# Recurrent mixer: the 64 token level's block products issued first, the 32 token level's directly behind them

## The chip, the cores and the metric

One core of one Trainium2 chip runs the whole program. The metric is the device time of one execution in microseconds (us). Matrix products run on TensorE (PE in the profile, its weight loads are PEld), elementwise work on VectorE (DVE), activations and copies on ScalarE (ACT), some elementwise work on GpSimd (POOL), and DMAs are issued mostly by SyncE (SP). Each engine works through its own queue in order; semaphores tie the queues together.

## The reference, cut to what matters

The model is an encoder trunk of two layers over 1024 tokens of width 1024. Layer 0 mixes tokens by windowed attention, layer 1 by a bidirectional gated linear recurrence (HGRN2); each layer also has four cross-attention heads and ends with a ConvGLU channel mixer. The change touches the recurrence of layer 1 alone:

```python
def gla_chunked(q, k, v, log_f):
    ...
    b = jnp.cumsum(log_f, axis=2)
    b_end = b[:, :, -1:]
    q_dec = q * jnp.exp(b)
    k_dec = k * jnp.exp(-b)
    k_end = k * jnp.exp(b_end - b)
    causal = np.tril(np.ones((HG_CHUNK, HG_CHUNK), dtype=bool))
    s = jnp.where(causal, jnp.einsum('bcthk,bcshk->bchts', q_dec, k_dec), 0.0)
    o_intra = jnp.einsum('bchts,bcshv->bcthv', s, v)

    def step(state, inp):
        qd, ke, vc, dec = inp
        o = jnp.einsum('bthk,bhkv->bthv', qd, state)
        state = dec[..., None] * state + jnp.einsum('bshk,bshv->bhkv', ke, vc)
        return state, o
    ...

o = (gla_chunked(q, k_f, v, lf_f)
     + flip_t(gla_chunked(flip_t(q), flip_t(k_b), flip_t(v), flip_t(lf_b))))
```

There are 8 heads of 128 keys and 128 values, a forward and a backward pass, and in each pass a token sees the values of the tokens before it (or behind it) weighted by a product of decays. The sums are exact whatever the chunk length is.

## The kernel before, in words

The program runs `start` (norms and memory keys), `window` (layer 0's mixer), an output projection, `ffn(0)`, then `hgrn` (layer 1's mixer), an output projection and `ffn(1)`. The tile framework orders each engine's queue when the program is built: a planner walks through time by a cost model, and of the instructions that are ready on an engine takes the one that stands earliest in the program text. An instruction of later text is taken where no earlier one is ready. The order that results is fixed in the program.

`hgrn` goes head by head (`head(h, cur)`, then `proj(h + 1)`). `proj` computes a head's queries `q`, forget inputs `f` and `b`, and for pairs of heads the values and gates, as products of the normed activations (`uh`, `ul`) with weights (`wh`, `wl`), in groups of 24 matmuls of 512 columns in fp32r into a PSUM tile `pj` (three matmuls per block: L84, L85, L86). Two `pj` banks exist. The rest of `hgrn` uses plain fp32, in which each `pe.matmul` becomes two instructions.

`head` calls `direction` four times, for (pass d, half b) = (0, 0), (1, 1), (0, 1), (1, 0); a half is 512 tokens, four blocks of 128. So there are 32 directions in all. One direction works like this, everything laid out as 128 keys by 512 tokens:

- ACT and DVE turn the forget input into log decays, sum them within chunks of 16 tokens (L1026) and take exponentials: `EP` (decay from the start of the chunk) and `ER` (decay to its end).
- L1054: four fp32 matmuls write the 128 by 128 score blocks `pa[:, c, :]` for chunks of 16 tokens and their pairs.
- The score blocks between further chunks are written over this by levels. For n = 32 and n = 64, `step(n // 2)` lengthens the decays (L1060 and L1061 on DVE, in place), then a tile `G` is filled, one half of it by POOL (L1068), the other by DVE (L1069), and L1074 multiplies its halves: for n = 32 there are 8 matmuls (16 instructions) that write 32 partitions each, for n = 64 there are 4 (8 instructions) that write 64 partitions each. They use a part of the array's columns, by `tile_position`. In the text the 32 token level stands first, and its matmuls stand ahead of `step(32)`.
- `step(64)`, then POOL takes out the total decay `dec` (L1080) and makes `qin` (L1082), to which DMAs of later weights are tied, and DVE makes `ER * k` (L1083).
- DVE copies the causal part of `pa` into `Az` (L1084), which ACT or POOL puts into `As` (L1088, L1090).
- PE transposes `ER * k` (L1093), ACT copies it (L1095), PE forms the state updates `pu` (L1098), and ACT and DVE run the states `S` (L1105, L1107).

After four directions `output` sums `po` from `As`, `qin` and `S` (L1122), norms and gates it and transposes it back (L1132). In heads 2, 4, 6 and 7 `cross` puts units of cross attention in between (transposes at L220, products through L84 to L86).

Tiles from `E()` share five buffers. A direction takes eight of them: `a_`, `L1`, `R`, `B`, `E1`, `E2`, and `G` of each level. A buffer is free again when the last reader of its tile is done; for a `G` that is the last matmul of its level at L1074. `pa` has two banks, shared with the scores of the cross attention.

Of the kernel before, what the change touches and what calls it, by code (L numbers as in the profile page):

```python
# [16 lines left out]
P = 128  # L17
# [32 lines left out]
def build(tc, A, out):  # L50
    nc = tc.nc
    act, dve, pool, pe = nc.scalar, nc.vector, nc.gpsimd, nc.tensor
# [824 lines left out]
    def hgrn():  # L877
# [4 lines left out]
        late = tc.alloc_tile_pool(name="hgv", bufs=1, side="right", reuse_waits="tile")  # L882
        V, G = [late.tile([P, 3, NT, P], F32, name=x) for x in ("v", "gs")]
        wp = tc.alloc_tile_pool(name="hg1", bufs=1, side="right", reuse_waits="tile")
# [4 lines left out]
        def bank(tag, shape=(P, 4, P)):  # L889
            return psp.tile(list(shape), F32, tag=tag, bufs=PB[tag], name=tag)  # L890
# [46 lines left out]
        def proj_tm(h, us, ts):  # L937
# [3 lines left out]
            for t in ts[::2]:  # L941
# [10 lines left out]
                for x in range(2):  # L952
                    g = G[:, two, t + x, :]
                    with tc.high_priority(AHEAD):
# [24 lines left out]
        def proj(h):  # L979

            r = {"q": [None, None], "s": [[None, None], [None, None]], "v": V[:, h % 3], "gs": G[:, h % 3], "marks": []}
            us = {}
# [21 lines left out]
        def direction(h, r, d, b, qin, S, As):  # L1004
# [5 lines left out]
            def E():  # L1010
                return early.tile([P, 512], F32, tag="E", bufs=5, name="E")

            def halves(x, n):
                x = x.rearrange("p (b a c) -> p b a c", a=2, c=n)
                return x[:, :, lt, :], x[:, :, er, :]
# [19 lines left out]
            pa = bank("pa")  # L1035
# [6 lines left out]
            def parts(n):  # L1042
                return halves(EP, n) + halves(ER, n) + halves(q, n) + halves(k, n)
# [12 lines left out]
            def step(n):  # L1056
                pl_, pe_, rl_, re_ = parts(n)[:4]
                e = 0 if d else n - 1
                nb = 512 // (2 * n)
                dve.tensor_tensor(re_, re_, bc(pl_[:, :, e:e + 1], [P, nb, n]), op=ALU.mult)  # L1060
                dve.tensor_tensor(pl_, pl_, bc(pe_[:, :, e:e + 1], [P, nb, n]), op=ALU.mult)  # L1061

            for n in (32, 64):
                step(n // 2)
                G = E()
                gl, ge = halves(G, n)
                pl_, pe_, rl_, re_, ql, qe, kl, ke = parts(n)
                pool.tensor_tensor(gl, pl_, ql, op=ALU.mult)  # L1068
                dve.tensor_tensor(ge, re_, ke, op=ALU.mult)  # L1069
                for c in range(4):  # L1070
                    for i in range(64 // n):
                        o = i * 2 * n
                        lo, eo = o + lt * n, o + er * n
                        pe.matmul(pa[eo:eo + n, c, lo:lo + n], G[:, c * P + eo:c * P + eo + n],  # L1074
                                  G[:, c * P + lo:c * P + lo + n], start=True, stop=True,
                                  tile_position=(0, eo))
            step(64)
            dec = wp.tile([P, 4], F32, tag="dec", bufs=2, name="dec")
            e = 0 if d else P - 1
# [71 lines left out]
        def head(h, r):  # L1151
            qin = [wp.tile([P, T], F32, tag=f"qin{d}", bufs=1, name="qin") for d in range(2)]
            S = [wp.tile([P, NT, P], F32, tag=f"S{d}", bufs=1, name="S") for d in range(2)]
            As = [None, None]
            for i, (d, b) in enumerate(((0, 0), (1, 1), (0, 1), (1, 0))):
                direction(h, r, d, b, qin[d], S[d], As)
                if i < len(r["later"]):
                    r["run"](r["later"][i])
                cross(HX[h][i])
                if h == 7 and i == 2:  # L1160
                    wo1.early(psj, 2, es)
            if h == 7:
                wo1.more(r["marks"], es)
                early.release()
                es.release()
                eq.release()
                wo1.w1 = tc.alloc_tile_pool(name="wa1", bufs=2, reuse_waits="tile")
                with tc.issue_after(r["marks"][2].ins):
                    wo1.load(0)
                wo1.open(2, 0)  # L1170
            for i, b in enumerate((1, 0)):
                output(h, r, b, qin, S, As)
                cross(HX[h][4 + i])
# [132 lines left out]
```

## Time and profile before

| | us |
|---|---|
| median of three runs (2729.33 to 2731.97) | 2729.53 |
| span of the profiled execution | 2732.3 |
| of it ahead of `hgrn` (to 1252) | 1252 |
| `hgrn` and the start of the output projection (1252 to 1940) | 688 |
| the rest (1940 to 2732) | 792 |
| PE busy over the span | 2661.3 |
| DVE busy | 1824.4 |
| ACT busy | 1391.2 |
| POOL busy | 468.6 |

The profiled execution's own span is 2.8 us above the median of the timed runs. Matmuls overlap in the pipeline: a matmul of 512 columns shows a duration of 0.39 us, while in a dense stretch the next one starts 0.227 us after it. What a matmul costs is read from the distance between starts, not from durations. In the timeline a row merges neighbours of one line; a row of L1074 gives the shape of its first instruction, so "128*32 ... x24" is a stretch that holds 16 instructions of the 32 token level and 8 of the 64 token level.

### The profile page before, as it was taken

The page shows a single profiled execution, that of the slowest core. Times are in us where ns is not written, and L with a number is a line of the kernel's source. Part 1 is how long each engine was busy: PE and PEld are TensorE (multiplying, and loading weights), DVE is VectorE, ACT ScalarE, POOL GpSimd, SP SyncE. Part 2 cuts the span into 40 slices and gives each one's busy share as a digit, 9 for nine tenths or more (in the row PEclk, how much of TensorE's full clock was granted, in tenths as well). Part 3 has the DMA queues.
Part 4 walks back from the last instruction along what each step waited for, and adds up shares of the span by engine and source line. Part 5 has one row for each costly group of instructions (what it writes and reads, how often), then busy time and mean ns, then how long its engine had stood idle before and what let it go on. Part 6 is the DMA issues. An engine that isn't in the chain of part 4 may idle for free.

```text
span 2732.3 us, 37483 instructions
## 1 busy us (share of the span) xinstructions
PE 2661.3 (97%) x13496; PEld 2231.1 (82%) x13496; DVE 1824.4 (67%) x3031; ACT 1391.2 (51%) x2550; POOL 468.6 (17%) x517
## 2 busy tenths in 40 slices
PE   8999999999999999999999999999899999999998
PEld 7888887788888888877888888888788788888886
DVE  6588777678556565488686767868566856556456
ACT  6367667544444445455444545545454544444453
POOL 1231120211111100032222231312121111110012
PEclk9999999999999999999999999999999999999999
DMA  8683213656777856673235531111466677775656
GB/s 282 207 186 75 66 49 97 204 183 154 199 205 187 206 155 232 204 249 124 86 124 127 117 78 55 55 47 34 133 219 170 165 202 204 197 206 159 222 192 219
DMA packets 213579, 428.45 MB, mean 157 GB/s; under 512 B 20368, under 2 KB 77072, under 8 KB 207760
## 3 DMA queue, kind: packets, MB, share of 16 engines
q1 hardware_dynamic: 187264, 333.50, 37.8%
q0 software_dynamic: 23680, 88.09, 15.6%
q10 hardware_dynamic: 2448, 4.46, 0.4%
q8 instruction: 106, 1.74, 0.3%
q14 instruction: 81, 0.66, 0.1%
HBM read 333.17 MB, written 117.96 MB: 165 GB/s over the span
## 4 chain that ended last, share of the span: by engine, by line
PE 84%; DVE 8%; DMA 3%; ACT 2%; issue 2%; POOL 1%; SPq 0%; DVEq 0%; POOLq 0%; ACTq 0%
PE X L541 25%; PE V L541 11%; PE pj L84 7%; PE pj L85 7%; PE pj L86 7%; PE Y L541 5%; PE pb L84 4%; PE pb L85 4%; PE pb L86 3%; PE po L1122 1%; PE pt L341 1%; PE pa L1074 1%; PE pa L1054 1%; DVE wl L80 1%; DVE wl L90 1%
## 5 line engine op out<-in xcount | busy, mean ns | idle before, releaser
L90 DVE TENSOR_TENSOR wl<-st,wh 128x1024 fp32r<-128x1024 f32 (+1 forms) x234 | 258.6, 1110 | 338.3 <-ACT wh L89 331.1
L89 ACT CAST wh<-st 128x1024 fp32r<-128x1024 f32 (+1 forms) x234 | 219.1, 938 | 291.4 <-PE X L541 180.4
L84 PE MATMUL pj<-uh,wh 128*128 128x512 f32 x512 | 206.6, 404 | 6.4 <-DVE xl L90 4.6
L541 PE MATMUL X<-wl,wh 128*128 128x512 f32 x528 | 205.6, 391 | 0.6 <-DVE wl L90 0.6
L541 PE MATMUL X<-wh,wl 128*128 128x512 f32 x528 | 205.7, 391 | 0.0
L541 PE MATMUL X<-wh 128*128 128x512 f32 x528 | 201.0, 391 | 4.0 <-DVE c L850 3.8
L86 PE MATMUL pj<-uh,wl 128*128 128x512 f32 x512 | 203.4, 398 | 0.0
L85 PE MATMUL pj<-ul,wh 128*128 128x512 f32 x512 | 202.7, 396 | 0.1
L84 PE MATMUL pj<-wh,uh 128*128 128x384 f32 (+1 forms) x512 | 190.2, 372 | 0.4 <-DVE v L283 0.4
L85 PE MATMUL pj<-wl,uh 128*128 128x384 f32 (+1 forms) x512 | 186.3, 364 | 0.0
L86 PE MATMUL pj<-wh,ul 128*128 128x384 f32 (+1 forms) x512 | 186.1, 364 | 0.0
L80 DVE TENSOR_TENSOR wl<-st,wh 128x1024 fp32r<-128x1024 f32 (+1 forms) x93 | 115.9, 1252 | 28.0 <-ACT wh L79 27.1
L541 PE MATMUL V<-uh,wh 128*128 128x512 f32 x344 | 133.9, 389 | 0.3 <-ACT uh L89 0.3
L541 PE MATMUL V<-ul,wh 128*128 128x512 f32 x344 | 134.0, 389 | 0.0
L541 PE MATMUL V<-uh,wl 128*128 128x512 f32 x344 | 133.9, 389 | 0.0
L79 ACT CAST wh<-st 128x1024 fp32r<-128x1024 f32 (+1 forms) x103 | 104.0, 1016 | 49.0 <-PE pj L85 27.2
L541 PEld LDWEIGHTS X<-wh 128*128 128x128 f32 x528 | 99.5, 189 | 25.9 <-issue 4.6
L84 PEld LDWEIGHTS pj<-uh,wh 128*128 128x128 f32 x512 | 97.3, 190 | 26.6 <-DVE xl L90 5.5
L1068 POOL TENSOR_TENSOR E<-EP,q 128x256 f32<-128x256 f32 x64 | 54.4, 851 | 372.0 <-DVE EP L1061 286.7
L541 PEld LDWEIGHTS X<-wl,wh 128*128 128x128 f32 x528 | 99.5, 189 | 21.9 <-DVE wl L90 1.0
L541 PEld LDWEIGHTS X<-wh,wl 128*128 128x128 f32 x528 | 99.4, 188 | 20.9
L86 PEld LDWEIGHTS pj<-uh,wl 128*128 128x128 f32 x512 | 97.0, 190 | 19.6
(337 smaller groups left out, 7328.7 us busy)
## 6 DMA issues: line engine op xcount, KB each, us to landing
st<-hid SPq DMA_DIRECT2D x154, 256.0 KB, 3.4
st<-in_ffw_dram SPq DMA_DIRECT2D x106, 256.0 KB, 3.5
w2s<-in_ffw_dram POOLq DMA_DIRECT2D x24, 1024.0 KB, 8.0
st<-in_ffw_dram SPq DMA_DIRECT2D x48, 512.0 KB, 3.7
hid<-tt SPq DMA_DIRECT2D x88, 256.0 KB, 4.6
st<-w2s SPq DMA_DIRECT2D x88, 256.0 KB, 3.2
sx<-in_ffw_dram SPq DMA_DIRECT2D x80, 256.0 KB, 4.0
sy<-in_ffw_dram SPq DMA_DIRECT2D x40, 512.0 KB, 5.8
```

Source lines behind the costliest of these rows:

```text
L79: act.copy(h[:, :n], raw)
L80: (eng or dve).tensor_tensor(l[:, :n], raw, h[:, :n].bitcast(F32), op=ALU.subtract)
L84: pe.matmul(o, ah, bh, start=first, stop=False)
L85: pe.matmul(o, ah, bl, start=False, stop=False)
L86: pe.matmul(o, al, bh, start=False, stop=last)
L89: act.copy(h, src)
L90: dve.tensor_tensor(l, src, h.bitcast(F32), op=ALU.subtract)
L341: pe.transpose(tp[:, j, :], sm[:, j, c * P:(c + 1) * P], ident)
L541: pe.matmul(o, x, y, start=new, stop=e, skip_group_check=not first)
L1054: pe.matmul(pa[:, c, :], E2[:, cs], E1[:, cs], start=True, stop=True)
L1068: pool.tensor_tensor(gl, pl_, ql, op=ALU.mult)
L1074: pe.matmul(pa[eo:eo + n, c, lo:lo + n], G[:, c * P + eo:c * P + eo + n], G[:, c * P + lo:c * P + lo + n], start=True, stop=True, tile_pos ...
```

## The change

The loop over n now only fills the two `G` tiles, with the same DVE and POOL instructions in the same text order as before. The matmuls move into a function `blocks(n)`, which is called for 64 first. `tc.issue_after(x)` adds an ordering edge, without a semaphore, from `x` to each instruction of the block that runs on the same engine: every matmul of the 32 token level comes behind the last one of the 64 token level in PE's queue. No instruction is added or taken away, and each matmul has the same operands and the same target as before.

```diff
+            Gs = {}
             for n in (32, 64):
                 step(n // 2)
-                G = E()
-                gl, ge = halves(G, n)
+                Gs[n] = E()
+                gl, ge = halves(Gs[n], n)
                 pl_, pe_, rl_, re_, ql, qe, kl, ke = parts(n)
                 pool.tensor_tensor(gl, pl_, ql, op=ALU.mult)
                 dve.tensor_tensor(ge, re_, ke, op=ALU.mult)
+
+            def blocks(n):
+                G = Gs[n]
                 for c in range(4):
                     for i in range(64 // n):
                         o = i * 2 * n
                         lo, eo = o + lt * n, o + er * n
-                        pe.matmul(pa[eo:eo + n, c, lo:lo + n], G[:, c * P + eo:c * P + eo + n],
-                                  G[:, c * P + lo:c * P + lo + n], start=True, stop=True,
-                                  tile_position=(0, eo))
+                        last = pe.matmul(pa[eo:eo + n, c, lo:lo + n], G[:, c * P + eo:c * P + eo + n],
+                                         G[:, c * P + lo:c * P + lo + n], start=True, stop=True,
+                                         tile_position=(0, eo))
+                return last
+
+            with tc.issue_after(blocks(64).ins):
+                blocks(32)
             step(64)
```

## The prediction

> **What bounds the kernel now.** I read the page's busy times and its chain first, then the table by stage, then PE's timeline inside `hgrn`.
>
> ```profile
> PE 2661.3 (97%) x13496; PEld 2231.1 (82%) x13496; DVE 1824.4 (67%) x3031; ACT 1391.2 (51%) x2550; POOL 468.6 (17%) x517
> PE 84%; DVE 8%; DMA 3%; ACT 2%; issue 2%; POOL 1%; SPq 0%; DVEq 0%; POOLq 0%; ACTq 0%
> 1252.00:1940.00 688.00, 678.13 (x4133) 568.97 (x4133) 516.28 (x1029) 346.97 (x757) 175.12 (x188) 1.00 0.28 81
> ```
>
> PE is busy 97% of the span and makes 84% of the chain that ended last. The third row is the stage of the change: PE is busy 678 of 688 us, DVE (the third pair) 516, ACT 347, POOL 175, and the granted clock is 1.00. So in this stage time follows what PE's queue costs, and a later result on DVE or ACT costs something only where PE then runs dry. Busy time can't show what a short matmul costs, since pipelined durations overlap. I read that from distances between starts in PE's timeline: how much later the stream of projections goes on when a stretch of L1074 stands in it.
>
> **What the change does to PE's queue.** No matmul comes or goes. What can change is in how many stretches the 24 instructions of a direction stand, and the order inside. Before, the 32 token level is ready several us ahead of the 64 token level, and the planner uses its matmuls to fill short holes. The first and the last stretch of the stage:
>
> ```profile
> 1280.20 0.31 PE L1074 MATMUL pa<-E 128*32 128x32 f32 x6
> ...
> 1929.65 0.92 PE L1074 MATMUL pa<-E 128*32 128x32 f32 x14
> ```
>
> Between these two the timeline shows L1074 in 58 stretches for 32 directions. 15 directions stand in one stretch of 24; the other 17 hold 26 boundaries too many. I counted three kinds: 10 cuts inside a level with projections between, 6 places where projections lie exactly between the two levels, and 10 cuts where only 128 column fp32 work (transposes, `po`) lies between.
>
> **The price of a stretch.** Four stretches between dense fp32r matmuls:
>
> ```profile
> 1279.65 0.39 PE L85 MATMUL pj<-ul,wh 128*128 128x512 f32 x1
> 1279.88 0.39 PE L86 MATMUL pj<-uh,wl 128*128 128x512 f32 x1
> ...
> 1280.44 0.50 PE L84 MATMUL pj<-wh,uh 128*128 128x512 f32 x1
> ...
> 1281.24 0.39 PE L84 MATMUL pj<-wh,uh 128*128 128x512 f32 x1
> ...
> 1284.42 0.39 PE L86 MATMUL pj<-wh,ul 128*128 128x512 f32 x1
> ```
>
> ```profile
> 1399.29 0.39 PE L86 MATMUL pj<-uh,wl 128*128 128x512 f32 x1
> 1399.52 1.05 PE L1054 MATMUL pa<-E 128*128 128x128 f32 x8
> 1400.50 0.45 PE L1074 MATMUL pa<-E 128*32 128x32 f32 x16
> ...
> 1401.68 0.39 PE L84 MATMUL pj<-uh,wh 128*128 128x512 f32 x1
> ```
>
> ```profile
> 1890.28 0.40 PE L85 MATMUL pj<-ul,wh 128*128 128x512 f32 x1
> 1890.60 0.68 PE L1074 MATMUL pa<-E 128*64 128x64 f32 x8
> ...
> 1892.01 0.40 PE L86 MATMUL pj<-uh,wl 128*128 128x512 f32 x1
> ```
>
> ```profile
> 1559.31 0.39 PE L86 MATMUL pj<-uh,wl 128*128 128x512 f32 x1
> 1559.53 1.05 PE L1054 MATMUL pa<-E 128*128 128x128 f32 x8
> 1560.52 1.05 PE L1074 MATMUL pa<-E 128*32 128x32 f32 x24
> 1561.50 0.50 PE L84 MATMUL pj<-uh,wh 128*128 128x512 f32 x1
> ...
> 1562.30 0.39 PE L84 MATMUL pj<-uh,wh 128*128 128x512 f32 x1
> ```
>
> The yardstick: from 1281.24 to 1284.42 there are 14 steps, so a dense projection matmul takes 0.227 us. A 128 column fp32 instruction takes 0.112 us, from this row of the chain (2.46 / 22):
>
> ```profile
> 1361.28 2.46 PE po L1122 x22
> ```
>
> In each case I take the time from the last projection ahead to the fourth behind, minus 4 x 0.227 = 0.91, minus 8 x 0.112 = 0.90 where L1054 stands in it. Six instructions of the 32 token level: 1281.24 - 1279.88 - 0.91 = 0.45. All 16: 1401.68 - 1399.29 - 0.91 - 0.90 = 0.58. The 64 token level's 8: 1892.01 - 1890.28 - 0.91 = 0.82. All 24 in one: 1562.30 - 1559.31 - 0.91 - 0.90 = 1.18. So each further instruction of 32 costs (0.58 - 0.45) / 10 = 0.013, and entering and leaving a stretch costs 0.45 - 6 x 0.013 = 0.37 us. Both levels apart cost 0.58 + 0.82 = 1.40 against 1.18 together: 0.22 saved where only the seam between the levels closes.
>
> For cuts with fp32 work between:
>
> ```profile
> 1716.43 1.05 PE L1054 MATMUL pa<-E 128*128 128x128 f32 x8
> 1717.41 0.38 PE L1074 MATMUL pa<-E 128*32 128x32 f32 x10
> 1717.72 0.66 PE L1132 MATMUL pt<-ident,on 128*128 128x128 f32 x4
> 1718.31 0.92 PE L1074 MATMUL pa<-E 128*32 128x32 f32 x14
> 1719.16 0.66 PE L1093 MATMUL pt<-ident,ER 128*128 128x128 f32 x4
> ```
>
> From L1054's start to the instruction behind the products: 1719.16 - 1716.43 - 12 x 0.112 = 1.39. Uncut, at 1559.53: 1561.50 - 1559.53 - 0.90 = 1.07. One such cut costs 0.3 us.
>
> If every direction stood whole: 10 x 0.37 + 6 x 0.22 + 10 x 0.3 = 8.0 us.
>
> **What of it is left.** The edge orders the levels, it doesn't glue them. The 32 token level follows at once only while nothing of earlier text is ready. Such an edge is in the kernel already, with a DMA tied to L1082:
>
> ```profile
> 1280.10 1.28 POOL L1082 TENSOR_TENSOR qin<-EP,q 128x512 f32<-128x512 f32 x1
> 1281.32 0.64 POOL L141 DMA_DIRECT2D w2s<-in_ffw_dram  x1
> ```
>
> The tied one follows directly. But the 64 token level is itself cut today in four directions, here into 2 and 6, with earlier text in between:
>
> ```profile
> 1876.09 0.56 PE L1074 MATMUL pa<-E 128*64 128x64 f32 x6
> ```
>
> That makes 4 cuts in 32 stretches of about 0.6 us. A group of 24 lasts 1.07 us, 1.75 times as long, so I expect 7 cuts at about 0.33: 2.3 us are not won. Sum: 8.0 - 2.3 = 5.7 us.
>
> **The new seam.** No row shows the 64 token level followed directly by the 32. Lower bound: the seam is free, and the 16 cost only 16 x 0.013 = 0.21 on top of 0.82, which is 0.15 less than 1.18; 32 x 0.15 = 4.8 us gained. Upper bound: it is as dear as two separate stretches, 0.22 more; 32 x 0.22 = 7.0 us lost. I take the nearest row, the seam in the other order at 1560.52: no change. The Trainium skill, "TensorEngine Tiling (Array Packing)", Key Properties, says that a change of tiling mode drains TensorE, while different tiles of one mode run beside each other. By that rule a stretch has three changes in either order, and the sum stays. The trace agrees with the drain at the entry: 0.32 us from the start at 1279.88 to 1280.20 where the pitch is 0.227.
>
> **What else moves, and its cover.** DVE's copy of `pa` (L1084) now waits for 24 instructions, where it waited for the 64 token level last. It is late by the 16 instructions and a seam, about 0.36 us, per direction. Behind it in DVE's queue stand the next direction's chain and the evacuation of `pj`. PE meanwhile has projections of the next head, so I cost this at nothing up to the last head, where no next head exists; there it is at most four times 0.36 us. `G` of the 32 token level stays until its matmuls are done, in the split directions some 5 us longer (a block of 24 projections is 24 x 0.227 = 5.4). The waits that already exist for these:
>
> ```profile
> DVE Az L1084 <- PE pa L1074: 7.6, 7, 3.5
> ACT E L1019 <- PE pa L1074: 14.6, 3, 5.0
> ```
>
> The next direction's `a_` and `L1` find a buffer once L1054 has freed `E1` and `E2`; by the time its own `E1` and `E2` are written, `a_`, `L1` and `R` are free again. Five buffers therefore hold both `G` and the next direction up to its products. The few extra waits fall on ACT, which is busy half the time: nothing, if PE stays fed. No DMA is moved: L1082 keeps its place on POOL. What comes late next is the cut copy of `pa` and with it `As`, which is needed only at the end of a head.
>
> **Rivals.**
>
> 1. *It stays cut.* Evacuation holes are short and the group is now longer; if 17 or more cuts of 0.33 remain, 5.6 us or more of the 8.0 are lost and the gain is about 2.4: 2727.1. For it: the holes that took 6 at 1280.20. Against: the 64 token level mostly stood whole.
> 2. *The seam is dear.* Half of the upper bound, 3.5 us lost: 2727.3 us.
> 3. *The reshuffle removes stalls,* or the seam is partly free. PE has one large stall in the stage:
>
> ```profile
> 1841.82 0.39 PE L86 MATMUL pj<-uh,wl 128*128 128x512 f32 x1
> 1844.35 0.50 PE L84 MATMUL pj<-uh,wh 128*128 128x512 f32 x1 [2.15 <-DVE xl L90]
> ...
> 1846.04 0.63 PE L84 MATMUL pj<-uh,wh 128*128 128x512 f32 x1
> 1846.47 0.63 PE L85 MATMUL pj<-ul,wh 128*128 128x512 f32 x1
> ...
> 1849.48 0.39 PE L84 MATMUL pj<-uh,wh 128*128 128x512 f32 x1
> ```
>
> PE waits 2.53 - 0.23 = 2.3 us for DVE, then matmuls start 0.43 apart instead of 0.227: 15 of them take 5.13 us where 3.41 are due, 1.7 us more. Such a stall costs 4.0 us. Without it the time would be 5.7 + 4.0 below: about 2719.8. The Trainium skill, "TensorE: Matmul & The Clock Gate", What's actually happening, has the array's clock halve after an idle window; the pitch of 0.43 agrees with the half.
>
> 4. *Held buffers starve PE (slower).* ACT can't start the next direction while a `G` of the 32 token level waits behind the 64. The evacuation of `pj` queues behind that chain on DVE, and PE runs dry as at 1844.35, at 4.0 us each. It decides from the third such stall on: 3 x 4.0 - 5.7 = 6.3 above, 2735.8. One or two leave the time within 0.2%. Against it: 15 directions already go in one stretch, and there projections go on behind it without a wait (1561.50).
>
> **How the numbers follow.** The working is against the profiled span of 2732.3; 5.7 less is 2726.6. That execution is 2.8 us longer than the median of 2729.53 and I keep the difference: 2723.8. Chances: forecast (about 2721 to 2727) 0.48; stays cut 0.20; dear seam 0.07; stalls removed or a free seam 0.14; starved 0.11. The range reaches from the third rival less 1.8 (a seam in part free as well) to the median plus 2 (two new stalls, or the seam's upper bound): 2718 to 2731.5. It leaves out the starved case and some tails. A measurement here tells 0.2%, about 5.5 us, from no change. The forecast lies on that line at 5.7, so its chance is split: faster 0.48 x 0.6 + 0.14 = 0.43, same the other 0.19 + 0.20 + 0.07 = 0.46, slower 0.11.
>
> **What would show it.** PE's timeline of the changed kernel: about 39 stretches of L1074 instead of 58, those of 24 beginning with 64 column instructions, each whole one costing 1.18 us between projections. Right in the sum if the stage 1252 to 1940 ends about 5.7 us earlier and everything ahead of 1252 is as it was. Wrong in the count if 50 or more stretches remain; wrong in the seam if a whole stretch costs 1.03 or 1.40. Starvation would show as waits of PE for DVE above 1 us and as matmul starts 0.43 apart at more places than 1846.

## The result, and the profile after

| | before | changed |
|---|---|---|
| median of the timed runs (us) | 2730.37 | 2735.06 |
| ratio, with its 95% interval | | 1.0016 [1.0009, 1.0023] |
| span of the profiled execution (us) | 2732.3 | 2729.4 |
| stretches of L1074 (L1078 in the changed kernel) on PE | 58 | 48 |

The changed kernel is slower by 0.16%, 4.4 us. That is less than the 0.2% I set as a difference, but its interval lies above 1, and it lies on the other side than the forecast of 2723.8; the measured median is also outside the range of 2718 to 2731.5. The two profiled executions stand the other way round (2729.4 against 2732.3). A single execution can't carry the comparison, and I come back to why.

The page and the table by stage of the changed kernel (in the last row: PE, PEld, DVE, ACT and POOL busy, granted clock, DMA):

```profile
PE 2654.7 (97%) x13496; PEld 2226.3 (82%) x13496; DVE 1822.1 (67%) x3031; ACT 1389.6 (51%) x2550; POOL 469.5 (17%) x517
PE 85%; DVE 8%; DMA 2%; ACT 2%; issue 2%; POOL 1%; SPq 0%; DVEq 0%; POOLq 0%; ACTq 0%
1252.00:1940.00 688.00, 674.18 (x4133) 566.31 (x4131) 514.89 (x1027) 345.95 (x757) 177.49 (x189) 1.00 0.28 80
```

PE has the same number of instructions and still makes most of the chain. Its order has changed as the edit says. PE's timeline of the changed kernel, the first stretches and the last:

```profile
1286.12 0.56 PE L1078 MATMUL pa<-E 128*64 128x64 f32 x6
1293.64 0.70 PE L1078 MATMUL pa<-E 128*64 128x64 f32 x18
...
1932.17 1.05 PE L1078 MATMUL pa<-E 128*64 128x64 f32 x24
```

The 64 column products lead everywhere. But the very first direction is cut again, now after 6 of the 64 token level's 8. The kernel before had stretches of 6 in this direction at 1280.20 and 1284.74; a hole that takes 6 is still there. Where a group stands whole, it costs what it cost before. Changed kernel first, then the kernel before:

```profile
1392.21 0.39 PE L84 MATMUL pj<-uh,wh 128*128 128x512 f32 x1
1392.53 1.05 PE L1078 MATMUL pa<-E 128*64 128x64 f32 x24
1393.51 0.65 PE L1101 MATMUL pt<-ident,ER 128*128 128x128 f32 x4
...
1394.70 0.40 PE L85 MATMUL pj<-ul,wh 128*128 128x512 f32 x1
```

```profile
1649.26 0.39 PE L86 MATMUL pj<-wh,ul 128*128 128x512 f32 x1
1649.58 1.05 PE L1074 MATMUL pa<-E 128*32 128x32 f32 x24
1650.56 0.66 PE L1093 MATMUL pt<-ident,ER 128*128 128x128 f32 x4
...
1651.75 0.40 PE L84 MATMUL pj<-uh,wh 128*128 128x512 f32 x1
```

From the last projection ahead to the fourth behind it is 2.49 us in both: 1394.70 - 1392.21 and 1651.75 - 1649.26. Over all whole groups that stand next to no wait (15 before, 19 in the changed kernel) the time above the dense pitches is 0.46 us in both. The new seam costs no more than the old one.

What got longer is PE's waiting. The view of waits, PE alone, in the stage; each row has the us in total, the number of waits and the longest. Before, then changed:

```profile
PE pj L84 <- DVE xl L90: 2.1, 1, 2.1
PE pj L84 <- DVE q L971: 1.7, 2, 1.4
PE pa L1054 <- DVE E L1051: 0.8, 2, 0.4
```

```profile
PE pj L84 <- DVE xl L90: 4.9, 3, 1.8
PE pj L84 <- DVE q L971: 3.1, 2, 1.7
PE pa L1054 <- DVE E L1051: 1.5, 3, 0.7
PE pj L84 <- DVE s L976: 0.4, 1, 0.4
```

A projection must wait until DVE has emptied a bank of `pj`: three times for `xl` (the cross attention's queries) instead of once, and for `q` twice as before, but longer.

**An account of PE.** The views give single waits; to set kernels against each other I added up all distances between starts on PE, from the first L1054 to the first matmul of `ffn(1)`. The work at dense pitches (0.227 us for 512 columns, 0.112 for 128 columns in fp32, 0.060 and 0.013 for the two levels) is 758.5 us in every kernel of this study. What is above it falls into: the edges of L1074's stretches; waits (a start more than 0.13 us late); matmuls at half clock; and the rest (inside of stretches and small delays). All in us; the time against the kernel before is the ratio of the timed runs times 2730.

| kernel | stretches | edges | waits | rest | sum of the three | half clock | sum against before | time against before, interval |
|---|---|---|---|---|---|---|---|---|
| before | 58 | 14.3 | 16.6 | 12.4 | 43.4 | 4.0 | | |
| changed | 48 | 11.8 | 21.5 | 12.3 | 45.6 | 0.2 | +2.2 | +4.4 [+2.5, +6.3] |
| again (changed) | 48 | 11.8 | 21.8 | 12.1 | 45.7 | 3.8 | +2.3 | +6.0 [+3.5, +8.5] |
| tie_plain | 52 | 12.5 | 22.6 | 11.5 | 46.6 | 4.0 | +3.2 | +5.5 [+3.0, +7.9] |
| tie_cross | 55 | 13.8 | 19.5 | 11.9 | 45.2 | 3.8 | +1.9 | +1.9 [-0.5, +4.4] |
| tie_h0 | 55 | 13.5 | 19.5 | 13.0 | 46.0 | 1.4 | +2.6 | +3.5 [+1.1, +5.7] |
| tie_h7 | 55 | 13.7 | 14.2 | 13.8 | 41.7 | 1.6 | -1.7 | -4.1 [-6.6, -1.6] |
| swap_exp | 59 | 14.7 | 12.7 | 12.7 | 40.0 | 1.6 | -3.3 | -3.5 [-6.0, -1.1] |
| a_swap | 47 | 11.7 | 19.0 | 11.5 | 42.2 | 2.6 | -1.2 | +0.3 [-1.9, +2.7] |
| a_hipri | 32 | 7.6 | 15.8 | 10.3 | 33.7 | 1.6 | -9.7 | -10.4 [-13.7, -6.8] |
| b_hipri | 36 | 8.2 | 14.6 | 11.0 | 33.8 | 1.4 | -9.5 | -11.2 [-14.5, -7.6] |
| a_hipri_swap | 32 | 8.3 | 12.8 | 11.0 | 32.2 | 0.2 | -11.2 | -10.4 [-14.2, -6.6] |
| b_hipri_swap | 37 | 8.7 | 10.3 | 10.5 | 29.5 | 1.4 | -13.9 | -12.0 [-15.3, -8.5] |

Three things are read here. The edges are 0.23 to 0.26 us per stretch in all thirteen profiles. The change won 2.5 us of edges and lost 4.9 us to waits; head by head the waits grew in heads 1 to 4, by 5.7 us in sum, and not in heads 6 and 7. And time spent at half clock differs by 3.6 us between two executions of the same program ("changed" and "again"), which is why one profiled span says little; the sum of the three leaves it out. With half clock the profile of the kernel before is the longer one in this stretch (43.4 + 4.0 against 45.6 + 0.2), without it the shorter one. In the kernel before it stands at 1846, as in the prediction's rows, and again from 1953 to 1958, behind the stage.

### The profile page after: what moved, and what is told of

Same layout as the page of the kernel before. It is cut to its first block, busy times and chain, and to the rows that moved or that the text cites. A ratio compares the mean times of both kernels' runs of the same rounds, so it can differ in the third digit from the quotient of the medians.

```text
span 2729.4 us, 37475 instructions
## 1 busy us (share of the span) xinstructions
PE 2654.7 (97%) x13496; PEld 2226.3 (82%) x13496; DVE 1822.1 (67%) x3031; ACT 1389.6 (51%) x2550; POOL 469.5 (17%) x517
## 3 DMA queue, kind: packets, MB, share of 16 engines
q0 software_dynamic: 23680, 88.09, 15.8%
## 4 chain that ended last, share of the span: by engine, by line
PE 85%; DVE 8%; DMA 2%; ACT 2%; issue 2%; POOL 1%; SPq 0%; DVEq 0%; POOLq 0%; ACTq 0%
PE X L541 26%; PE V L541 11%; PE pj L84 7%; PE pj L85 7%; PE pj L86 7%; PE Y L541 5%; PE pb L84 4%; PE pb L85 4%; PE pb L86 3%; PE po L1130 1%; PE pt L341 1%; PE pa L1078 1%; PE pa L1054 1%; PE pt L119 1%; PE pu L1106 1%
```

## The experiments

**Again.** The changed kernel, unaltered.

> The changed kernel once more, unaltered, for a second profile. Theory A (PE runs dry: in the heads with cross attention the evacuation of the projection banks now comes later in DVE's queue than PE needs it): the waits of PE for DVE's xl (L90) and q (L971) that the first profile of the changed kernel shows, 1.5 to 2.1 us each at five places, come back at the same places, since the order is fixed in the program; time 2 to 6 us above the kernel before. Rival B (the difference between the kernels is that of single executions, no property of the order): the waits move by more than 1 us, and the time is within 2 us of the kernel before.

Measured: 2737.18 us, ratio 1.0022 [1.0013, 1.0031]. PE's timeline of this second profile shows the waits of the first at the same places:

```profile
1410.80 0.50 PE L84 MATMUL pj<-uh,wh 128*128 128x512 f32 x1 [1.40 <-DVE q L971]
1508.15 0.50 PE L84 MATMUL pj<-uh,wh 128*128 128x512 f32 x1 [1.23 <-DVE xl L90]
1583.72 0.51 PE L84 MATMUL pj<-uh,wh 128*128 128x512 f32 x1 [1.72 <-DVE q L971]
1681.28 0.80 PE L84 MATMUL pj<-uh,wh 128*128 128x512 f32 x1 [1.84 <-DVE xl L90]
1855.45 0.50 PE L84 MATMUL pj<-uh,wh 128*128 128x512 f32 x1 [1.82 <-DVE xl L90]
```

In the first they were 1.41 at 1411.03, 1.71 at 1583.95, 1.85 at 1681.51. Two of the five, 1.23 and 1.40, are shorter than the 1.5 that was expected, but none moved. The orders of PE, DVE and ACT are the same in both profiles, instruction by instruction. So the waits belong to the program's order; rival B falls.

**tie_plain and tie_cross.** The change in a part of the heads; the others issue each level's products inside the loop as before.

```diff
+            tied = h in (0, 1, 3, 5)
...
+                if not tied:
+                    blocks(n)
...
-            with tc.issue_after(blocks(64).ins):
-                blocks(32)
+            if tied:
+                with tc.issue_after(blocks(64).ins):
+                    blocks(32)
```

tie_cross has (2, 4, 6, 7) in the first line.

> The change in heads 0, 1, 3 and 5 alone, which have no cross attention; heads 2, 4, 6 and 7 as before. 52 stretches of the levels' products are planned instead of 58. Theory A: no new wait for xl; 6 stretches fewer at 0.33 us give 2 us, time 1 to 3 us below the kernel before. Theory C (any other plan of the stage is as good or bad as the changed one, wherever the edit stands): 2 to 6 us above it, with waits at new places.

> The change in heads 2, 4, 6 and 7 alone, those with cross attention; heads 0, 1, 3 and 5 as before. 55 stretches planned instead of 58. Theory A: the waits for xl of the changed kernel are there again, at least two of 1.5 us or more, and the time is 3 to 7 us above the kernel before (the whole loss of the changed kernel and none of the gain of heads 0, 1, 3, 5). Theory C: 2 to 6 us above as well, but with waits at other places than in the changed kernel.

Measured: tie_plain 2735.77 us, 1.0020 [1.0011, 1.0029]; tie_cross 2732.68 us, 1.0007 [0.9998, 1.0016]. Theory A predicted the opposite order and falls as it was put; tie_cross has one wait for `xl` above 1.5 us, not two. Theory C holds for tie_plain (5.5 us); for tie_cross, at 1.9 us, it isn't decided. In tie_plain the text of heads 2 and 4 is that of the kernel before, and still both get a new wait for `xl`:

```profile
1510.65 0.50 PE L84 MATMUL pj<-uh,wh 128*128 128x512 f32 x1 [2.14 <-DVE xl L90]
1687.20 0.50 PE L84 MATMUL pj<-uh,wh 128*128 128x512 f32 x1 [2.14 <-DVE xl L90]
```

The edit in one head moves what the planner does in the next ones.

**tie_h0 and tie_h7.** The same with `tied = h in (0,)` and `tied = h in (7,)`.

> The change in head 0 alone (4 of 32 directions), 55 stretches planned. Theory R: the orders of DVE and ACT differ from the kernel before well beyond head 0, and waits of PE for xl or q change by 1 us or more in heads 1 to 6, where the text is as before; time between 1 below and 5 above the kernel before. Rival T: 3 stretches fewer, waits change in head 0 alone, time 0 to 2 us below.

> The change in head 7 alone, the last one; up to head 6 the order of all engines is that of the kernel before. 55 stretches planned. Theory R: the waits of heads 0 to 6 are those of the kernel before to within 0.2 us each, and only 3 x 0.25 us and what happens in head 7 count: time within 2 us of the kernel before. Rival T: the buffers held cost most here, since no next head fills PE: 2 us or more above it, with waits of PE in head 7.

Measured: tie_h0 2735.21 us, 1.0013 [1.0004, 1.0021]; tie_h7 2727.37 us, 0.9985 [0.9976, 0.9994]. In tie_h0 theory R holds: 3.5 us, with new waits in heads 2 and 3, whose text is as before. PE's timeline, with the longest wait for `xl` of the study, in head 2:

```profile
1508.57 0.70 PE L84 MATMUL pj<-uh,wh 128*128 128x512 f32 x1 [3.11 <-DVE xl L90]
1509.06 0.63 PE L85 MATMUL pj<-ul,wh 128*128 128x512 f32 x1
1509.49 0.63 PE L86 MATMUL pj<-uh,wl 128*128 128x512 f32 x1
```

The two rows behind it start 0.43 us apart: a spell of half clock follows this wait. tie_h7, edited in the last head alone, keeps the waits of the kernel before up to there:

```profile
1411.21 0.50 PE L84 MATMUL pj<-uh,wh 128*128 128x512 f32 x1 [1.36 <-DVE q L971]
...
1846.37 0.50 PE L84 MATMUL pj<-uh,wh 128*128 128x512 f32 x1 [2.14 <-DVE xl L90]
```

In the kernel before they were 1.36 at 1409.18 and 2.15 at 1844.35. tie_h7 became faster, by 4.1 us where theory R allowed 2 (the interval reaches down to 1.6). Its waits fell by 2.5 us. Up to head 6 they are those of the kernel before to within 0.2 us a head, and DVE's order is the same up to 1892; what fell lies in head 7 and behind it. That buffers held back cost most in the last head (rival T) is refuted.

**swap_exp and a_swap.** Two neighbouring ACT instructions swapped in the kernel before (swap_exp) and in the changed one (a_swap). They are independent, and no matmul is touched.

```diff
-            act.activation(e1, Re, AF.Exp, scale=-1.0)
             act.activation(l2, Bl, AF.Exp, scale=-1.0)
+            act.activation(e1, Re, AF.Exp, scale=-1.0)
```

> The kernel before with two neighbouring ACT instructions of a direction swapped (L1046 and L1047), which neither adds work nor changes what PE gets; the planner makes another order of it from there on, with 59 stretches instead of 58. Theory R (any new plan of the stage draws its own waits of PE, and the kernel before stands at the good end of them): stretches cost the same, waits of PE in the stage between 17 and 23 us where the kernel before has 16.6, time 0 to 6 us above it. Rival T (the loss comes from holding the 32 token level back): nothing is held back here, so waits and time within 1.5 us of the kernel before.

> The changed kernel with the same two ACT instructions swapped as in swap_exp; to be set against swap_exp (0.9987 of the kernel before) as the changed kernel is against the kernel before. 47 stretches planned against 59. Theory R (the levels' order saves 0.25 us for each stretch saved; the waits of PE are drawn anew with each plan and have no tie to the levels' order): edges of stretches 12 x 0.25 = 3 us below swap_exp; waits of PE anywhere from 13 to 23 us, so the time against swap_exp is not bound to be +4 us again, and the waits for xl and q come at other places than in the changed kernel. Rival T (holding the 32 token level back is what costs): waits 4 to 6 us above those of swap_exp (12.7), at the changed kernel's places, and the time 2 to 6 us above swap_exp.

Measured: swap_exp 2727.95 us, 0.9987 [0.9978, 0.9996]; a_swap 2730.26 us, 1.0001 [0.9993, 1.0010]. Waits of PE in swap_exp (its three largest rows), then in a_swap:

```profile
PE pb L84 <- ACT oh L89: 3.0, 3, 1.4
PE pu L85 <- DVE pl L90: 1.0, 1, 1.0
PE pj L84 <- DVE gs L957: 0.8, 1, 0.8
```

```profile
PE pj L84 <- DVE q L971: 3.5, 2, 2.1
PE pb L84 <- ACT oh L89: 2.0, 1, 2.0
PE pu L1106 <- ACT kT L1103: 1.6, 1, 1.6
```

A swap that changes no matmul takes 4 us of waits away: the long waits for `xl` and `q` are gone. So theory R is right that a plan draws its own waits, and wrong in that the kernel before stood at the good end of them. Rival T, which allowed 1.5 us, falls here too. a_swap against swap_exp has edges 3.0 us lower, as predicted, and waits 6.4 us higher. Most of its waits stand at other places than the changed kernel's (for `kT`, and hardly for `xl`), which speaks for R; but their sum rises as rival T said it would. I take both results as they are: with the 64 token level first, waits are longer in both plans.

**a_hipri and b_hipri, and the same with the swap.** The products of both levels are planned ahead of earlier text, in the changed order and in the order of before.

```diff
+            with tc.high_priority(AHEAD):
+                last = blocks(64)
+                with tc.issue_after(last.ins):
+                    blocks(32)
```

```diff
+                with tc.high_priority(AHEAD):
+                    for c in range(4):
+                        for i in range(64 // n):
...
```

> The changed kernel, with the products of both levels planned ahead of all earlier text once they are ready. All 32 directions then stand whole: 32 stretches instead of 48. If a cut costs what the rows of the prediction gave (0.33 us) and nothing else moves, 16 cuts fewer give 5.3 us below the changed kernel, about 1 us below the kernel before. Theory A adds that the waits for xl stay unless the new plan happens to move the evacuations. Rival D (cuts are cheap because they stand where PE would wait anyway): no gain against the changed kernel.

> The kernel before, its order of the levels kept (32, then 64), with the products of both levels planned ahead of all earlier text once they are ready. 36 stretches are planned instead of 58. Theory W (what counts is in how many stretches the products stand, at about 0.25 us each, as the first five kernels' accounts show, and not which level is first): 22 x 0.25 = 5.5 us below the kernel before, and within 3 us of the kernel with the priority and the changed order (2721.5). Rival O (the order with 64 first is what brought that kernel's gain): within 2 us of the kernel before.

> The changed order, planned ahead of earlier text, with the two ACT instructions swapped: 32 whole stretches. Theory R: edges as in a_hipri (7.6 us), waits drawn anew; time within 5 us of a_hipri on either side, below the kernel before in any case.

> The order of before, planned ahead of earlier text, with the two ACT instructions swapped: 37 stretches. Theory R: edges about 8.4 us, waits drawn anew; within 5 us of b_hipri on either side; if the waits of swap_exp (12.7) could be had together with whole stretches, 2 us below b_hipri.

Measured: a_hipri 2721.49 us, 0.9962 [0.9950, 0.9975]; b_hipri 2720.38, 0.9959 [0.9947, 0.9972]; a_hipri_swap 2720.50, 0.9962 [0.9948, 0.9976]; b_hipri_swap 2718.45, 0.9956 [0.9944, 0.9969]. All four beat both kernels, the kernel before by 10 to 12 us. In a_hipri the first direction, which stood cut in both other kernels, is whole:

```profile
1289.73 1.05 PE L1078 MATMUL pa<-E 128*64 128x64 f32 x24
```

Against the kernel before, b_hipri's edges are down by 6.1 us, its waits by 2.0 and the rest by 1.4: 9.5 of the 11.2 us. So theory W holds for the edges (5.5 us expected) and for the order, and rival O falls: whole stretches pay, and the order of the levels doesn't pay by itself. W has no account of the other half of the gain. In a_hipri too, the sum of the three is 11.9 us below that of the changed kernel where 5.3 were expected: 4.2 of edges, 5.7 of waits, 2.0 of the rest. A new plan draws new waits, so what came from them can't be put down to whole stretches. Rival D, cuts that cost nothing, falls. The four pairs that differ in the order of the levels and in what it holds back (before and changed, swap_exp and a_swap, b_hipri and a_hipri, with the swap and without) all have longer waits with 64 first: by 4.9, 6.4, 1.2 and 2.5 us.

## Why the prediction was wrong

- *PE is the bound of the stage, and time is what its queue costs:* right. The work was 758.5 us in every profile, and the sums of edges, waits and rest follow the timed differences, to within 4 us and with the right sign in all kernels but a_swap, which is even.
- *The seam costs nothing in the new order:* right, as the two rows of 24 show. The drain that the Trainium skill tells of ("TensorEngine Tiling (Array Packing)", Key Properties) fits: a group has three changes of tiling in either order, and both groups take 2.49 us with their neighbours.
- *The price of a cut,* 0.37 and 0.3 us: about right, as far as it can be told. The account's edges are 0.25 us per stretch, but a part of what a stretch costs lies inside of it and is booked under the rest. In a_hipri every direction stands whole, and edges and rest together are 8.8 us below the kernel before, where the prediction gave 8.0 for that state: 0.34 for each of the 26 stretches fewer. Between the kernel before and the changed one it is 2.6 us for 10, or 0.26 each. The rest also holds delays that have nothing to do with cuts, so these figures are rough.
- *What of it is left:* 7 cuts were to remain; 16 did (48 - 32), nearly what my first rival put as its condition. I scaled today's cuts of the 64 token level by duration. But a cut comes where earlier text becomes ready in the middle of a group (planned ahead of that text, as in a_hipri, all 32 directions stand whole), and a group of 24 was cut far more often than its length let me expect. So 10 x 0.25 = 2.5 us were won instead of 5.7, most of it lost by the count and not by the price.
- *What else moves, and its cover:* this step failed, and it turned the sign: put at nothing, it measured 4.9 us of added waits. I cost everything on DVE and ACT at nothing because PE has other projections to do. But those projections need a free bank of `pj`, and DVE frees it in the order that the planner wrote. With another order on PE the planner wrote another order for DVE too: the two kernels' orders on DVE part in head 0, at 1295.76 in the kernel before. Head 4 shows what it costs. DVE's timeline of the changed kernel at the wait that ended at 1681.51:

```profile
1678.64 0.43 DVE L1061 TENSOR_TENSOR EP<-EP 128x256 f32<-128x256 f32 x1
1678.99 0.42 DVE L1070 TENSOR_TENSOR E<-ER,s 128x256 f32<-128x256 f32 x1
1679.32 0.34 DVE L1115 SCALAR_TENSOR_TENSOR S<-S,dec,pu 128x128 f32<-128x128 f32 x1
1679.58 0.68 DVE L207 TENSOR_REDUCE nm<-ps 128x2 f32<-128x512 f32 x1
1680.18 0.41 DVE L1060 TENSOR_TENSOR ER<-ER,EP 128x256 f32<-128x256 f32 x1
1680.51 0.34 DVE L1115 SCALAR_TENSOR_TENSOR S<-S,dec,pu 128x128 f32<-128x128 f32 x1
1680.77 0.68 DVE L90 TENSOR_TENSOR xl<-pj,xh 128x512 fp32r<-128x512 f32 x1
```

ACT's `xh` is ready at 1678.93, but `xl` stands behind six other instructions until 1680.77, and PE waits. `xh` itself came late: it has one buffer, which the scores of the unit before still read on PE until about 1677.5. In the kernel before these scores were done, and `xh` began, at about 1670.1, more than 3 us ahead of L1054. The kernel before at this place, the row of `xl` from DVE's timeline first, then PE's:

```profile
1673.46 0.68 DVE L90 TENSOR_TENSOR xl<-pj,xh 128x512 fp32r<-128x512 f32 x1
```

```profile
1673.80 1.16 PE L1054 MATMUL pa<-E 128*128 128x128 f32 x8 [0.46 <-ACT xp L211]
1674.89 0.45 PE L1074 MATMUL pa<-E 128*32 128x32 f32 x16
1675.27 0.50 PE L84 MATMUL pj<-uh,wh 128*128 128x512 f32 x1
```

There `xl` ran from 1673.46 to 1674.14, so the bank was free before the 32 token level's products began at 1674.89, and the projection followed them without a wait. In the changed kernel `xl` is late, and for 1.5 us of the wait the same products were complete but held behind the 64 token level: they could have filled a part of it.

- *How much the filler is:* in the changed kernel 3.0 to 3.6 us of PE's waits, by how they are counted, fall into times when a direction's tile of the 32 token level was complete and its products not yet issued; in the kernel before 1.4 us. So at most 2.2 of the 4.9 us come directly from work held back; in a_swap it is 1.4 against 0.8 in swap_exp, of 6.4 us. The larger part, by difference, is when results and banks come free, which the order of all engines sets.
- *The fourth rival* had the place right, evacuation behind other work on DVE with PE running dry. It had the price wrong: the added waits are 0.6 to 2.0 us, not 4.0, since half clock doesn't follow each of them. Its mechanism, a held `G` that starves ACT, isn't what the runs show: ACT's waits for a buffer that the levels' products free are 14.6 us before and 15.3 us changed, waits of PE appear in heads whose text is as before, and the edit in the last head alone made it faster. ACT's waits for a buffer that L1054 frees did grow, from 15.5 to 24.6 us; whether they reach PE wasn't tested.

Shown: the edges of a stretch cost about 0.25 us, the order of the levels inside a whole group is neutral in price, and the waits belong to the plan and move with edits elsewhere. Open: why the waits are longer with 64 first in all four pairs, beyond the filler; four plans are few, and an order with DVE's and ACT's queues pinned to those of before wasn't tried. Open as well: 2 to 4 us of the changed kernel's timed loss, which the account of one profile doesn't hold. Time at half clock varies by that much from execution to execution, and the timed runs' mean granted clock points there: 0.9935 in 27 runs of the kernel before, 0.9926 and 0.9916 in the 21 and 11 runs of the changed one, and within each group the slower runs tend to have the lower clock. That longer waits bring more half clock would fit, but isn't shown.

## What to carry to other kernels

A cost that is paid per interruption is best removed by making the group uninterruptible for the planner (here a priority: 0.4% faster, with about half of it from the stretches and the rest from the new plan's waits and small delays), not by moving one half behind the other and hoping that they stay together. Where a planner writes the queues of all engines, an edit to one engine's order rewrites the others too: set a neutral swap beside the change before a few us are put down to it. And small products that look like interruptions can fill a wait; ask what PE does there once they are held back.

## What the runs showed of the hardware

Leaving and entering the narrow column tiles costs the same in sum from either level: a group of 24 took 2.49 us with its neighbours in both orders. Full width products in plain fp32 cost no such edge: 54 times in the trace of the kernel before, 2 to 28 of them stand between products of 512 columns without a wait, and the time is that of the pitches of 0.112 and 0.227 us to within 0.03 us. A wait of PE can be followed by matmuls at half pitch (0.43 instead of 0.227 us): it was behind 3.11 us of idle time at 1508.57 in tie_h0, and behind 1.84 us at 1681.28 in the changed kernel's second execution, but not behind 1.85 us at the same place in its first. In all, that program lost 0.2 us by it in one execution and 3.8 us in the other. The Trainium skill, "TensorE: Matmul & The Clock Gate", What's actually happening, says that the activity window runs free of the kernel's start, which fits that the same wait is followed by half clock in one execution and not in the next.
